# More weight slots, later stores of the low parts, and splits on GpSimd in a two-sequence encoder

## The chip, the cores and the metric

The kernel runs on one core of a Trainium2 chip. The metric is the device time of one execution, in microseconds. PE is TensorE, DVE VectorE, ACT ScalarE, POOL GpSimd, and SP is SyncE, which issues nearly all of this kernel's transfers.

## What is computed

Two sequences of 512 tokens, 1024 wide, go through the same two layers with the same weights.

```python
def encoder_trunk(x, p):
    for l in range(DEPTH):                                   # 2
        h = rms_norm(x, p['ln1_g'][l])
        z = h @ p['w_in'][l]                                 # 1024 -> 2816
        z_s5, z_hy, z_rw, z_na = jnp.split(z, IN_SPLITS, axis=-1)
        y_s5 = s5_mixer(z_s5, ...)                           # state-space scan
        y_hy = hyena_mixer(z_hy, ...)                        # long convolution
        y_rw = rwkv_mixer(z_rw, ...)                         # RWKV-7, both directions
        y_na = na_mixer(z_na, ...)                           # neighbourhood attention
        groups = [rms_norm(y, p['grp_g'][l, i]) for i, y in enumerate((y_s5, y_hy, y_rw, y_na))]
        x = x + jnp.concatenate(groups, axis=-1) @ p['w_out'][l]      # 1024 -> 1024
        h = rms_norm(x, p['ln2_g'][l])
        x = x + jnp.square(jax.nn.relu(h @ p['w_mlp1'][l])) @ p['w_mlp2'][l]   # 1024 -> 4096 -> 1024
    return x
y_prompt, y_sample = encoder_trunk(x_prompt, p), encoder_trunk(x_sample, p)
```

All of it is in float32.

## The kernel before

**Dense matmuls in three products.** A float32 operand is written as the sum of two numbers of the type fp32r, a high part and a low part. A dense product is then three matmuls, high by high, high by low and low by high (`mm3`: L1433 and L1434 read the weight's high part, L1435 its low part). `K.split` (L298 to L301) makes the parts: ScalarE casts the number to the high part (L300), and an engine that the caller names subtracts (L301) to get the low part.

**Weights come in tiles** of 512 by 128 numbers, 256 KB, 128 partitions by 512 elements in SBUF; one tile serves 12 matmuls of 512 columns. `load_w` (L1401) loads one. The first sequence meets each tile first: SyncE loads the raw tile into a low slot (L1419), ScalarE casts it into a high slot (L300), VectorE subtracts in place (L301), and SyncE stores the low part to DRAM (L1423). For the second sequence SyncE loads the raw tile (L1415) and the stored low part (L1416), and ScalarE casts in place (L1417). There are 376 tiles, so 376 first and 376 second loads. `NW` slots of 2 KB a partition hold them; the constants `NW, NHI = 7, 3` stand at L1835. A first load takes high slot `n % NHI` and low slot `NHI + n % (NW - NHI)`, a second load two slots in a ring over all `NW`; n counts loads.

**Activations** live in the rest of SBUF, `NMEM` units of 1 KB a partition, of which the dense stream has the first `DHI`; `DS5` bounds the S5 mixer's part (L1833). `Mem` hands out units and prefers ones that were freed long ago. `take` (L1707) splits a mixer's output into one tile of 8 units for each of the four groups, and `w_out` (L1544) reads them.

**Three streams of Python generators** write the program down side by side: the dense stream, the RWKV stream with S5 and the later mixers, and a first stream with preparation and the first mixers. The dense stream's order is: w_in of layer 0 for sequence 0 and for sequence 1; then for each layer and sequence w_out, MLP, and w_in of the next layer. While it works on one sequence, the mixers of the other run. A planner then lays out each engine's queue and SyncE's from these, by its own costs and by priorities; the dense matmuls have a lower priority than the mixers' (`OFF_P`). Each queue runs in that order. Semaphores are set from what the instructions read and write.

**Where the mixers touch this.** L442, L447 and L454 are GpSimd instructions of RWKV's preparation, the last of them ahead of the matmuls at L470. L551 makes the operands of the matmuls at L564, L668 scales RWKV's state, L959 and L604 are matmuls on data just loaded (S5's operands, RWKV's values). L1596 adds a matmul's result from PSUM to the MLP's sum, L1457 adds squares for a normalisation. `LO_V` (L1836) is not used.

Of the kernel before, what the change touches and what calls it, by code (L numbers as in the profile page):

```python
# [5 lines left out]
F32 = mybir.dt.float32  # L6
F32R = mybir.dt.float32r
# [5 lines left out]
P = 128  # L13
T = 1024
S = 512
# [1385 lines left out]
def load_w(K, key):  # L1401


    nc = K.nc
    sh = [P, 4, P]
    src = K.A[key[0]][key[1:]]
    n = K.nw
    K.nw += 1
    again = key in K.lows
    i, j = (2 * n % NW, (2 * n + 1) % NW) if again else (n % NHI, NHI + n % (NW - NHI))  # L1410
    hi, lo = (K.W.view(NMEM + 2 * o, sh, F32R) for o in (i, j))
    raw = K.W.view(NMEM + 2 * (i if again else j), sh, F32)
    K.tc.cur_priority -= OFF_W
    if again:
        nc.sync.dma_start(out=raw, in_=src)  # L1415
        nc.sync.dma_start(out=lo.bitcast(F32), in_=K.lows[key])  # L1416
        nc.scalar.copy(out=hi, in_=raw)  # L1417
    else:
        nc.sync.dma_start(out=raw, in_=src)  # L1419
        K.split(hi, lo, raw, nc.vector)  # L1420
        K.n += 1
        d = K.lows[key] = K.d(sh, f"lo_{K.n}")
        nc.sync.dma_start(out=d, in_=lo.bitcast(F32))  # L1423
    K.tc.cur_priority += OFF_W
    return hi, lo


def mm3(K, ps, terms):

    n = len(terms)  # L1430
    K.tc.cur_priority += OFF_P
    for i, (wh, wl, hh, hl) in enumerate(terms):
        K.nc.tensor.matmul(out=ps, lhsT=wh, rhs=hh, start=(i == 0), stop=False)  # L1433
        K.nc.tensor.matmul(out=ps, lhsT=wh, rhs=hl, start=False, stop=False)  # L1434
        K.nc.tensor.matmul(out=ps, lhsT=wl, rhs=hh, start=False, stop=(i == n - 1))  # L1435
    K.tc.cur_priority -= OFF_P


def dense(K, key, h, tag="pd"):

    w = [load_w(K, key + (kh,)) for kh in range(2)]
    ps = K.p([P, S], tag)
    mm3(K, ps, [(w[k // 4][0][:, k % 4], w[k // 4][1][:, k % 4], h[k][0], h[k][1]) for k in range(8)])
    return ps
# [99 lines left out]
def w_out(K, l, khs, ys, xsrc, xp, done, M):  # L1544


    nc = K.nc
    load = not xp
    for m in range(8):
        if load and m % 2 == 0:  # L1550
            xp.append(M([P, 2, S]))
        x = xp[m // 2][:, m % 2]
        if load:
            nc.sync.dma_start(out=x, in_=xsrc[m * P:m * P + P])
        w = [load_w(K, ('w_out', l, m, kh)) for kh in khs]
        ps = K.p([P, S], "pd")
        mm3(K, ps, [(w[i][0][:, j], w[i][1][:, j]) + tuple(ys[HALVES[kh][j // 2]][:, part, j % 2] for part in range(2))
                    for i, kh in enumerate(khs) for j in range(4)])
        nc.vector.tensor_tensor(out=x, in0=ps, in1=x, op=ADD)
        if done:  # L1560
            done(m, x, xp[m // 2])
        yield
    M.free(*(ys.pop(g) for kh in khs for g in HALVES[kh]))


def mlp(K, l, h, R2, xd, done, M):
# [15 lines left out]
    def second(e):  # L1582
        for m in range(8):
            if e == 0 and m % 2 == 0:
                acc.append(M([P, 2, S]))
            if e == 7 and m % 2 == 0:
                xp.append(M([P, 2, S]))
                nc.sync.dma_start(out=xp[-1], in_=xd[m * P:m * P + 2 * P].rearrange("(c p) t -> p c t", p=P))
            a = acc[m // 2][:, m % 2]
            wh, wl = load_w(K, ('w_mlp2', l, m, e))  # L1590
            ps = K.p([P, S], "pd")
            mm3(K, ps, [(wh[:, j], wl[:, j], hid[4 * e + j][:, 0], hid[4 * e + j][:, 1]) for j in range(4)])
            if e == 0:
                nc.scalar.copy(out=a, in_=ps)
            else:
                nc.vector.tensor_tensor(out=a, in0=ps, in1=a, op=ADD)  # L1596
            if e == 7:
                x = xp[-1][:, m % 2]
                nc.vector.tensor_tensor(out=a, in0=a, in1=R2, op=MUL)
                nc.vector.tensor_tensor(out=x, in0=a, in1=x, op=ADD)  # L1600
                done(m, x)
                if m % 2:
                    M.free(acc[m // 2], xp[-1])
            yield
        for j in range(4):
            M.free(hid.pop(4 * e + j))
# [46 lines left out]
def trunk(tc, A, O):  # L1653
    nc = tc.nc
    base = place(nc)
    with tc.tile_pool(name="sb", bufs=1) as sb, \
            tc.tile_pool(name="ps", bufs=1, space=bass.MemoryType.PSUM) as ps, \
            tc.tile_pool(name="dr", bufs=1, space=bass.MemoryType.DRAM) as dr:
        K = Ctx(tc, base, sb, ps, dr, A)
        K.s5w, K.hys, K.lows, K.nw, K.nz = {}, {}, {}, 0, 0  # L1660
        K.W = K.mem()

        DM, MX = K.mem((0, DHI)), K.mem((DHI, NMEM))
# [7 lines left out]
        zs, ys, taken, done = {}, {}, {}, set()  # L1671
# [19 lines left out]
        def into(l, b, h, st, DM):  # L1691
            R = norm_rstd(K, st, DM)
            zs[l, b] = (K.d([D, S], f"zr{b}", 2), K.d([16, 16, 8, 64], f"zd{b}", 2), K.d([768, S], f"zh{b}", 2),
                        K.d([768, S], f"zn{b}", 2))
            ys[l, b] = {}
            for i, _ in enumerate(w_in(K, l, pars[l], h, R, zs[l, b], FIRST[:] if l + b == 0 else None)):
                if i == 7:
                    done.add(("zr", l, b))
                    if b == 0 and l and len(ys[l - 1, 1]) == 4:
                        take(l - 1, 1)  # L1700
                    if b == 1 and l and len(ys[l, 0]) == 4:
                        take(l, 0)
                yield
            DM.free(*h)
            done.add(("z", l, b))

        def take(l, b, gs=range(4)):  # L1707

            t = taken.setdefault((l, b), {})
            for g in gs:  # L1710
                y, my = ys[l, b][g]
                t[g] = DM([P, 2, 2, S], F32R)
                K.split(t[g][:, 0], t[g][:, 1], y, nc.vector)
                my.free(y)
            if 2 in t:
                done.add(("freed", l, b))

        def layer(l, b):
# [10 lines left out]
            for khs in (((0,), (1,)) if l + b < SPL else ((0, 1),)):  # L1729
                gs = [g for kh in khs for g in HALVES[kh]]  # L1730
                while not all(g in ys[l, b] for g in gs):
                    yield
                if not done.issuperset([("freed", l, b)]):
                    take(l, b, gs)
                    yield
                yield from w_out(K, l, khs, taken[l, b], xs[l, b], x0, None if khs == (0,) else mid, DM)
# [93 lines left out]

NMEM, DHI, DLO, DS5 = 164, 84, 41, 144  # L1833

NW, NHI = 7, 3  # L1835
OFF_D, LO_V, MIX = 0, 4, 2  # L1836
FN, OFF_M, OFF_W, OFF_P, OFF_R = 2, 0, 0, 2000, 0
ACC_V, NF = 6, 4
# [1 line left out]
HALVES = ((1, 3), (0, 2))  # L1840
# [44 lines left out]
```

## Time and profile before

| | |
|---|---|
| median of 3 runs | 3182.41 us (3180.72 to 3187.07) |
| the profiled execution's own time | 3182.62 us |
| its span, first to last instruction | 3180.8 us |
| mean granted clock of TensorE, of 1 | 0.949 |
| PE busy | 2964.7 us, 93% |
| DVE busy | 1935.5 us, 61% |
| ACT busy | 1128.3 us, 35% |
| POOL busy | 453.6 us, 14% |
| DMA | 588.70 MB, 185 GB/s on the mean |

The span begins with the first instruction and ends with the last; 1.8 us of the execution lie outside it. A busy PE counts the time from a matmul's start to its modelled end, and matmuls overlap, so it is not PE at its peak. Stages are told apart by the weights that SyncE loads: the first load of w_out is issued at 464.19 us, of the MLP of layer 0 at 623.87 for the first sequence and at 1393.81 for the second, of w_out of layer 1 at 2109.79 and at 2742.85, of the MLP of layer 1 at 2211.59 and at 2816.53. The stages in the rows begin a little before these. [...]

### The profile page before, as it was taken

What the parts mean: (1) busy time and instruction counts of PE and PEld (TensorE: products, weight loads), DVE (VectorE), ACT (ScalarE), POOL (GpSimd) and SP (SyncE); (2) the same over time, 40 slices, a digit from 0 to 9 for tenths busy, and PEclk for the clock granted to TensorE, in tenths of its full rate; (3) what the DMA queues carried; (4) which work ended last, traced back from release to release, by engine and by line L of the source; (5) the groups of instructions that cost most, each with busy time, mean ns of one, the idle gap of its engine ahead of it and who ended that gap; (6) DMA issues with size and microseconds to landing.
All of it is one profiled execution on the core that took longest, in us unless ns stands there. A gap on an engine that the chain in (4) does not pass through costs nothing. (4 is left out here: it accounts for less than half of the span.)

```text
span 3180.8 us, 48627 instructions
## 1 busy us (share of the span) xinstructions
PE 2964.7 (93%) x17328; PEld 2317.7 (73%) x17328; DVE 1935.5 (61%) x3909; ACT 1128.3 (35%) x2080; POOL 453.6 (14%) x411
## 2 busy tenths in 40 slices
PE   7978999899999999999999899988999999799999
PEld 5666776677777867777777677866777777588887
DVE  7987783874874697653844527668547467731223
ACT  4333233443332343244332324333433333343332
POOL 3422210200100022211101002213000001100000
PEclk9988997899999999999999999989999999899999
DMA  7577564464565566774764655666646555466666
GB/s 220 184 228 189 172 188 142 139 169 158 163 194 168 188 204 202 240 236 155 207 174 145 182 169 196 218 200 187 177 139 169 174 178 185 155 215 194 194 192 215
DMA packets 491801, 588.70 MB, mean 185 GB/s; under 512 B 188678, under 2 KB 239494, under 8 KB 490536
## 3 DMA queue, kind: packets, MB, share of 16 engines
q1 hardware_dynamic: 491560, 585.59, 60.1%
q8 instruction: 139, 2.28, 0.3%
q14 instruction: 102, 0.84, 0.1%
HBM read 418.34 MB, written 164.22 MB: 183 GB/s over the span
## 5 line engine op out<-in xcount | busy, mean ns | idle before, releaser
L1433 PE MATMUL pd<-m,m 128*128 128x512 f32 x2984 | 1222.0, 410 | 63.8 <-ACT m L300 23.4
L1435 PE MATMUL pd<-m,m 128*128 128x512 f32 x2984 | 1205.7, 405 | 22.5 <-DMA m<-lo 15.7
L1434 PE MATMUL pd<-m,m 128*128 128x512 f32 x2984 | 1205.8, 404 | 1.6 <-DVE m L301 1.4
L1433 PEld LDWEIGHTS pd<-m,m 128*128 128x128 f32 x2984 | 578.3, 194 | 214.2 <-ACT m L300 27.8
L1435 PEld LDWEIGHTS pd<-m,m 128*128 128x128 f32 x2984 | 577.9, 194 | 166.3 <-DMA m<-lo 19.5
L1434 PEld LDWEIGHTS pd<-m,m 128*128 128x128 f32 x2984 | 579.1, 194 | 131.2 <-issue 8.4
L300 ACT CAST m<-m 128x512 fp32r<-128x512 f32 (+1 forms) x400 | 256.4, 644 | 619.9 <-PE pd L1434 220.6
L1417 ACT CAST m<-m 128x512 fp32r<-128x512 f32 x376 | 232.2, 619 | 612.9 <-DMA m<-in_w_mlp 362.4
L301 DVE TENSOR_TENSOR m<-m,m 128x512 fp32r<-128x512 f32 (+1 forms) x400 | 303.1, 761 | 203.4 <-ACT m L300 198.1
L1596 DVE TENSOR_TENSOR m<-pd,m 128x512 f32<-128x512 f32 x224 | 153.9, 688 | 205.4 <-PE pd L1435 204.5
L1578 DVE SCALAR_TENSOR_TENSOR do<-pd,do 128x512 f32<-128x512 f32 x128 | 88.0, 687 | 202.4 <-ACT do L1577 201.9
L1196 DVE TENSOR_TENSOR m<-m,m 128x512 f32<-128x512 f32 (+1 forms) x224 | 125.6, 601 | 6.5 <-PE ma L1375 4.8
L301 DVE TENSOR_TENSOR m<-do,m 128x512 fp32r<-128x512 f32 x128 | 88.2, 689 | 50.0 <-ACT m L300 49.2
L300 ACT CAST m<-do 128x512 fp32r<-128x512 f32 x128 | 79.4, 621 | 98.7 <-DVE do L1578 98.5
L1577 ACT ACTIVATE do<-pd 128x512 f32<-128x512 f32 x128 | 75.9, 593 | 37.6 <-PE pd L1435 37.3
L668 POOL TENSOR_TENSOR rw_se<-rw_st,rw_ec 128x256 f32<-128x256 f32 x24 | 15.8, 659 | 484.1 <-DVE rw_st L669 361.9
L470 PE MATMUL ra<-m,m 64*128 64x128 f32 x512 | 63.1, 308 | 21.8 <-DVE m L454 10.3
L1196 POOL TENSOR_TENSOR m<-m,m 128x512 f32<-128x512 f32 x32 | 49.0, 1534 | 234.7 <-DVE m L1196 77.7
L1457 POOL TENSOR_TENSOR m<-m 128x512 f32<-128x512 f32 x40 | 59.8, 1494 | 152.9 <-ACT m L1456 150.9
L863 POOL TENSOR_TENSOR m<-m,s5p_i 128x256 f32<-128x256 f32 x64 | 61.7, 963 | 135.7 <-DVE m L865 71.4
L678 PE MATMUL ra<-m,m 128*64 128x64 f32 x512 | 78.8, 248 | 1.3 <-DVE m L653 0.9
L470 PEld LDWEIGHTS ra<-m,m 64*128 64x128 f32 x512 | 54.3, 206 | 34.9 <-issue 24.3
(363 smaller groups left out, 3505.6 us busy)
## 6 DMA issues: line engine op xcount, KB each, us to landing
m<-in_w_mlp SPq DMA_DIRECT2D x512, 256.0 KB, 2.9
lo<-m SPq DMA_DIRECT2D x376, 256.0 KB, 2.6
m<-lo SPq DMA_DIRECT2D x376, 256.0 KB, 2.7
m<-in_w_in SPq DMA_DIRECT2D x176, 256.0 KB, 3.2
m<-zr SPq DMA_DIRECT2D x36, 512.0 KB, 4.8
m<-in_w_out SPq DMA_DIRECT2D x64, 256.0 KB, 3.5
m<-in_xT SPq DMA_DIRECT2D x32, 256.0 KB, 4.3
zr<-do SPq DMA_DIRECT2D x32, 256.0 KB, 2.4
```

The costliest lines, as they stand in the source:

```text
L300: self.nc.scalar.copy(out=hi, in_=x)
L301: eng.tensor_tensor(out=lo, in0=x, in1=hi.bitcast(F32), op=SUB)
L470: nc.tensor.matmul(out=pm[q][:, ch - c2, c], lhsT=bk[c][h, ch].rearrange("p a b -> p (a b)"), rhs=ar[c][h, ch].rearrange("p a b -> p (a b) ...
L678: nc.tensor.matmul(out=py[b0:b0 + 64, d, c], lhsT=uv[:, ch, c, q], rhs=sr[:, ch, 2 * c + q], start=st is None, stop=True)
L1196: eng.tensor_tensor(out=o, in0=a, in1=b, op=op)
L1417: nc.scalar.copy(out=hi, in_=raw)
L1433: K.nc.tensor.matmul(out=ps, lhsT=wh, rhs=hh, start=(i == 0), stop=False)
L1434: K.nc.tensor.matmul(out=ps, lhsT=wh, rhs=hl, start=False, stop=False)
L1435: K.nc.tensor.matmul(out=ps, lhsT=wl, rhs=hh, start=False, stop=(i == n - 1))
L1577: nc.scalar.activation(out=r, in_=ps, func=AF.Relu)
L1578: nc.vector.scalar_tensor_tensor(out=r, in0=ps, scalar=0.0, in1=r, op0=MAX, op1=MUL)
L1596: nc.vector.tensor_tensor(out=a, in0=ps, in1=a, op=ADD)
```

## The change

It has four parts. The weights get eleven slots instead of seven, four of them for high parts; the activations get 8 units less, all of them from the dense stream's region. The store of a low part is no longer written right behind its split but after the load of the tile two later; before a second load all pending stores are written. The subtraction of a first load goes to GpSimd in three of four cases. And a mixer's output is split into two tiles of 4 units instead of one of 8.

```diff
     K.tc.cur_priority -= OFF_W
     if again:
+        store_lows(K)
         nc.sync.dma_start(out=raw, in_=src)
         nc.sync.dma_start(out=lo.bitcast(F32), in_=K.lows[key])
         nc.scalar.copy(out=hi, in_=raw)
     else:
         nc.sync.dma_start(out=raw, in_=src)
-        K.split(hi, lo, raw, nc.vector)
-        K.n += 1
-        d = K.lows[key] = K.d(sh, f"lo_{K.n}")
-        nc.sync.dma_start(out=d, in_=lo.bitcast(F32))
+        K.split(hi, lo, raw, nc.vector if K.nw % LO_V == 0 else nc.gpsimd)
+        K.late.append((key, lo))
+        store_lows(K, 2)
     K.tc.cur_priority += OFF_W
     return hi, lo
+
+def store_lows(K, n=0):
+    while len(K.late) > n:
+        key, lo = K.late.pop(0)
+        K.n += 1
+        d = K.lows[key] = K.d([P, 4, P], f"lo_{K.n}")
+        K.nc.sync.dma_start(out=d, in_=lo.bitcast(F32))
...
-        mm3(K, ps, [(w[i][0][:, j], w[i][1][:, j]) + tuple(ys[HALVES[kh][j // 2]][:, part, j % 2] for part in range(2))
+        mm3(K, ps, [(w[i][0][:, j], w[i][1][:, j]) + tuple(ys[HALVES[kh][j // 2]][part][:, j % 2] for part in range(2))
...
-    M.free(*(ys.pop(g) for kh in khs for g in HALVES[kh]))
+    M.free(*(t for kh in khs for g in HALVES[kh] for t in ys.pop(g)))
...
-        K.s5w, K.hys, K.lows, K.nw, K.nz = {}, {}, {}, 0, 0
+        K.s5w, K.hys, K.lows, K.late, K.nw, K.nz = {}, {}, {}, [], 0, 0
...
-                t[g] = DM([P, 2, 2, S], F32R)
-                K.split(t[g][:, 0], t[g][:, 1], y, nc.vector)
+                t[g] = [DM([P, 2, S], F32R) for _ in range(2)]
+                K.split(*t[g], y, nc.vector)
...
-NMEM, DHI, DLO, DS5 = 164, 84, 41, 144
+NMEM, DHI, DLO, DS5 = 156, 76, 41, 136
...
-NW, NHI = 7, 3
+NW, NHI = 11, 4
 OFF_D, LO_V, MIX = 0, 4, 2
```

## Rows read from the trace of the kernel before

**Rows 1.** By stage: busy us (x instructions) of PE, PEld, DVE, ACT, POOL; clock; DMA.
```profile
460.00:622.00 162.00, 149.81 (x1104) 111.78 (x1103) 96.14 (x214) 60.69 (x131) 17.12 (x18) 0.80 0.50 146
622.00:1154.00 532.00, 501.82 (x3207) 392.00 (x3206) 350.94 (x689) 185.75 (x353) 57.04 (x47) 0.97 0.58 175
...
1394.00:1937.00 543.00, 515.68 (x3136) 390.26 (x3137) 271.27 (x527) 189.49 (x341) 56.92 (x52) 0.96 0.60 179
...
2108.00:2210.00 102.00, 83.23 (x514) 68.35 (x513) 91.92 (x225) 32.28 (x55) 29.39 (x20) 0.85 0.59 188
2210.00:2740.00 530.00, 506.34 (x3143) 394.68 (x3142) 324.04 (x609) 188.90 (x367) 41.44 (x41) 0.97 0.57 172
2740.00:2815.00 75.00, 56.00 (x254) 46.26 (x253) 41.80 (x76) 20.21 (x32) 12.56 (x9) 0.84 0.55 173
2815.00:3180.00 365.00, 359.69 (x1589) 296.59 (x1587) 98.83 (x145) 123.89 (x209) 1.29 (x1) 1.00 0.62 200
sum 3180.00, PE 2964.72 PEld 2317.70 DVE 1935.47 ACT 1128.25 POOL 453.59; mean PE 247.06 PEld 193.14 DVE 161.29 ACT 94.02 POOL 37.80
```

**Rows 2.** TensorE's waits, whole span: us in total, times, longest.
```profile
PE pd L1433 <- ACT m L300: 23.4, 9, 12.3
PE ra L564 <- DVE m L551: 20.8, 7, 4.4
PE pd L1435 <- DMA m<-lo: 15.7, 9, 3.8
...
PE ma L959 <- DMA m<-s_sB: 11.7, 5, 4.9
...
PE ra L470 <- DVE m L454: 10.3, 5, 6.3
...
PE ra L470 <- DVE m L453: 7.5, 6, 4.0
...
PE pd L1435 <- DVE m L301: 6.7, 5, 3.3
PE pd L1433 <- ACT m L1417: 6.4, 1, 6.4
...
PE ra L604 <- DMA m<-zr: 2.8, 2, 1.5
```

**Rows 3.** TensorE's waits in the stage 0 to 207.
```profile
PE pd L1433 <- ACT m L300: 12.3, 1, 12.3
```

**Rows 4.** SyncE's own waits, whole span.
```profile
SPq L1416 <- PE pd L1434: 628.0, 274, 27.2
SPq L1419 <- PE pd L1435: 372.3, 199, 6.8
SPq L1423 <- DVE m L301: 274.3, 226, 6.2
```

**Rows 5.** Waits of all engines, whole span.
```profile
DVE m L301 <- ACT m L300: 247.3, 189, 7.0
ACT m L300 <- PE pd L1434: 220.6, 102, 9.4
```

**Rows 6.** Line L301: duration ns min/median/max, first and last start.
```profile
L301 DVE TENSOR_TENSOR m<-m,m x400: 654/690/1836, 16.1 to 2777.9; 128x512 fp32r<-128x512 f32 x127, 128x1024 fp32r<-128x1024 f32 x7
```

**Rows 7.** Line L1596, the same columns.
```profile
L1596 DVE TENSOR_TENSOR m<-pd,m x224: 662/691/702, 756.9 to 3175.6; 128x512 f32<-128x512 f32 x112
```

**Rows 8.** Line L1457, the same columns.
```profile
L1457 POOL TENSOR_TENSOR m<-m x40: 1267/1456/2404, 6.5 to 2816.2; 128x512 f32<-128x512 f32 x40
```

**Rows 9.** GpSimd's groups by line: busy us, mean ns, idle before.
```profile
L447 POOL TENSOR_TENSOR m<-m,m 128x512 f32<-128x512 f32 x16 | 29.9, 1871 | 14.4 <-DVE m L445 11.5 <-ACT m L431 2.9
L454 POOL TENSOR_TENSOR m<-m,m 64x512 f32<-64x512 f32 x16 | 24.5, 1529 | 1.3
L442 POOL TENSOR_TENSOR m<-m,m 128x512 f32<-128x512 f32 x16 | 24.2, 1514 | 87.5 <-ACT m L431 87.4
```

**Rows 10.** DMA issues: count, KB each, median us to landing.
```profile
xm<-m SPq DMA_DIRECT2D x32, 256.0 KB, 4.3
```

## The prediction

> **What bounds the kernel now.** I read the table by stage first [rows 1]. The line of sums shows TensorE busy for 2964.7 of 3180 us, VectorE for 1935.5, ScalarE for 1128.3, GpSimd for 453.6: TensorE is the bound, and all that better supply can give back is its idle time of 215 us, plus what the clock loses where it is below 1.00. The rows above the sums say where that lies. The first sequence's MLP of layer 0 (622 to 1154) takes 532 us and the second's (1394 to 1937) 543, although the first does the splits and the second reads finished low parts: how the low parts are made does not set the pace of an MLP, because mixers of another pair of sequence and layer share TensorE with it. The last MLP, alone on the engine, takes 365 us. Three stages have idle time and a low clock together: 460 to 622 (clock 0.80), 2108 to 2210 (0.85) and 2740 to 2815 (0.84). There the dense work is short and the mixers' chains run bare.
>
> Then the waits of TensorE by releaser [rows 2]. Those that a weight ends are short: 23.4 us for a high part of a first load, 15.7 for a low part read back, 6.7 for a low part from the split, 6.4 for a high part of a second load. Of the first, 12.3 us is a single wait in the opening stage [rows 3], when nothing is loaded yet; slots cannot help it. The mixers' own waits stand beside them: 20.8 us at L564, 10.3 and 7.5 at L470, and 11.7 and 2.8 for mixer data still being loaded.
>
> The queue that issues the loads looks much worse than what reaches TensorE [rows 4]: SyncE waits 628.0 us to issue the read of a low part until the slot's last matmul is over, 372.3 to issue a first load for the same reason, and 274.3 us at L1423 until the split that it is to store is done. Behind each of these waits stand all later transfers, the mixers' too. In the engines' queues the same shows [rows 5]: VectorE idles 247.3 us before a split until ScalarE has made the high part, and ScalarE idles 220.6 us before that cast until matmuls free a high slot. So the chain load, cast, split, store is tight, but TensorE mostly has other work in front of it meanwhile.
>
> **The change, part by part.**
>
> *Eleven slots.* A second load uses two of them, so 5.5 tiles fit where 3.5 did; a first load has 4 high and 7 low slots instead of 3 and 4. A tile is 12 matmuls; in the last MLP 128 tiles take 365 us, 2.85 us each [rows 1]. Two more tiles ahead are 5.7 us of lead. Against that stand the second sequence's waits, 15.7 + 6.4 = 22.1 us [rows 2]. I take all of it: -22; the bounds are -22 and 0 (if the wait merely moves to the next thing in TensorE's queue). For the first sequence the waits are 23.4 - 12.3 + 6.7 = 17.8 us [rows 2, 3]. The fourth high slot loosens the cast, but the split becomes longer (below), so I take half: -9, between -18 and 0.
>
> *Stores two tiles later.* The same 376 stores are issued, each behind the load of the tile after the next. SyncE no longer holds at a split that is only just starting, so of the 274.3 us most goes; the waits for a slot's matmul stay, though with seven low slots they start later [rows 4]. What TensorE sees of this queue is late mixer data: 11.7 + 2.8 = 14.5 us [rows 2]. I take half: -7, between -14.5 and 0. The low slot is held longer by the late store, which three more slots cover; the memory in DRAM is read back a whole stage later. These two I cost at nothing; without the extra slots each load would wait for a store two tiles on.
>
> *Splits on GpSimd.* 376 splits are first loads; their numbers start at multiples of four, so exactly 282 move. VectorE has a median of 690 ns for this line [rows 6], so it is relieved of 282 x 0.690 = 195 us. GpSimd's addition of the same form has a median of 1456 ns and a minimum of 1267 [rows 8], so it takes on 282 x 1.456 = 411 us (at least 357) and goes from 454 to about 865 us, 27% of the span. In the stage 2210 to 2740, 96 of 128 splits move: 140 us more, on top of 41.4, is 181 of 530 us, about a third [rows 1]. Behind a split that waits for its cast now stand GpSimd's mixer instructions. Nearest to TensorE are the three ahead of L470: L442, L447 and L454, sixteen of each [rows 9]. I estimate that half of the sixteen rounds fall beside first-sequence stages. If each of these instructions met one split, that is 8 x 3 x 1.456 = 35 us; by the third of the time that GpSimd is busy, 12 us. I take +12, between 0 and +35.
>
> VectorE's relief should shorten the mixers' chains: waits on VectorE at L564 and L470 are 20.8 + 10.3 + 7.5 = 38.6 us [rows 2], and it would no longer stand 247.3 us before splits [rows 5]. But the two engines are not independent. The same split line has a median of 690 ns and a maximum of 1836 on VectorE [rows 6], while additions that read one operand from PSUM stay between 662 and 702 in all 224 cases [rows 7]; GpSimd's additions spread from 1267 to 2404 [rows 8]. Something makes an instruction with both inputs in SBUF wait up to 1.15 us, about one GpSimd instruction. So I cost this at nothing, between -19 (half of the 38.6) and +19: the 195 us that VectorE saves stand against up to 411 us in which its two-input instructions may be shut out.
>
> [...]
>
> *Less room for activations.* The dense stream's region goes from 84 units to 76. The fullest moment is the end of an output projection: 32 units of mixer output, 32 of normalised activations, 4 for the statistics and 4 for a pair of x tiles, 72 in all, which fits, with one spare pair instead of three. New x pairs then land where an older pair was just stored, and a store takes 4.3 us [rows 10]. Twelve pairs in three such stages are 52 us at worst, but the loads are issued ahead of their matmuls, which cover them; I cost this at nothing, and it widens the range upwards. Splitting the mixer output into two tiles each changes no instruction's work.
>
> *Order.* The program's planner lays out every queue from its own costs, so all queues are laid out anew. I have no row for that; the clock can go either way by half of what it loses in the three bare stages: 162 x 0.20 + 102 x 0.15 + 75 x 0.16 = 60 us [rows 1], so 30 us to either side.
>
> **Sum.** -22 - 9 - 7 + 12 = -26 us. The profiled execution took 3182.6 us, 1.8 outside its span, and the median of the runs is 3182.4, the same. 3182.6 - 26 = 3156.6: I predict 3157 us.
>
> **Rivals.**
>
> *GpSimd becomes the hold-up (slower).* Place: the first sequence's stages, where GpSimd's splits sit in front of L442, L447 and L454 and shut VectorE out of its two-input work. Then the 35 us come whole, the 9 us for the first sequence do not come, and the 38.6 us of mixer waits on VectorE grow by half, +19: -22 - 7 + 35 + 19 = +25, 3208 us. It decides from the point where GpSimd costs TensorE more than the 22 + 7 = 29 us that slots and queue give. For it: the maxima in [rows 6, 8]. Against it: GpSimd has two thirds of its time left, and VectorE no longer stands before splits.
>
> *Nothing comes of it.* TensorE's queue is in fixed order; a weight that comes earlier lets it arrive earlier at a mixer matmul that is not ready, and the idle time changes its name. For it: the two MLP stages of 532 and 543 us. Then about 3183 us.
>
> *The bare stages shrink.* If mixers finish earlier because VectorE is freed, the three stages named lose half their idle time, (12.2 + 18.8 + 19.0) / 2 = 25 us, and half the clock loss, 30 us; 7 of it is the late mixer data counted above: -26 - 55 + 7 = -74, 3109 us. For it: TensorE's longest mixer waits are on VectorE [rows 2]. Against it: the second of the stages has splits of its own, on the slower engine.
>
> **Numbers.** The forecast's case gets 0.40, with 3135 to 3175 as its own range; GpSimd as hold-up 0.28; nothing 0.13; the bare stages 0.19. A difference of 0.2% (6 us) is about what a measurement of this kernel can tell from no change. Faster by more than that: 0.40 + 0.19 = 0.59; within it 0.13; slower 0.28. The range reaches from somewhat under the third rival to just over the first, 3100 to 3212; outside are all gains together with a better clock, and a hold-up on GpSimd together with late x pairs or a worse clock.
>
> **What the profile of the changed kernel would show.** If the steps are right: the waits for low parts read back and for L1417 all but gone from TensorE's list; SyncE's wait at the store under 100 us; VectorE busy about 195 us less, GpSimd about 411 more, at some 1.45 us a split; L470's waits on GpSimd longer by about 12 us. If GpSimd is the hold-up: TensorE waits for a low part from GpSimd, splits well over 1.5 us, VectorE's two-input lines with a higher mean than now. The prediction is wrong if TensorE's idle time does not fall though the weight waits do, or if the clock in the three bare stages moves by more than a tenth.

## The result, and the profile after

The changed kernel takes 3212.1 us in the median of four runs (3206.7 to 3219.4) against 3184.7 us for four runs of the kernel before, timed beside it: a ratio of 1.0072, with a 95% interval of 1.0048 to 1.0095. It is slower by 0.7%. The forecast was 3157 us, so the time moved the other way; the rival that ends nearest is the one with GpSimd as the hold-up, 3208 us.

First the table by stage of the changed kernel, with the columns of [rows 1]; the borders are set where its stages begin. Left out are four stages.

```profile
210.00:440.00 230.00, 204.80 (x1394) 159.27 (x1394) 155.84 (x349) 74.37 (x142) 50.44 (x52) 0.90 0.66 189
440.00:690.00 250.00, 190.63 (x1364) 145.89 (x1362) 172.53 (x402) 73.20 (x154) 54.48 (x45) 0.73 0.42 115
690.00:1241.00 551.00, 518.76 (x3288) 404.03 (x3288) 330.77 (x634) 192.83 (x373) 193.78 (x153) 0.97 0.56 172
...
1490.00:2034.00 544.00, 527.20 (x3302) 411.03 (x3300) 278.06 (x574) 195.63 (x382) 53.11 (x51) 0.95 0.58 175
...
2217.00:2273.00 56.00, 51.36 (x416) 40.16 (x417) 30.23 (x45) 23.02 (x46) 19.85 (x15) 0.94 0.88 272
2273.00:2790.00 517.00, 500.00 (x2963) 394.20 (x2961) 288.00 (x508) 179.49 (x344) 178.53 (x139) 0.98 0.54 170
2790.00:2841.00 51.00, 47.77 (x200) 38.26 (x199) 31.14 (x38) 19.09 (x30) 8.31 (x6) 0.97 0.82 273
2841.00:3212.00 371.00, 365.36 (x1615) 301.43 (x1613) 100.75 (x147) 125.03 (x211) 2.58 (x2) 1.00 0.62 198
sum 3212.00, PE 2974.15 PEld 2327.53 DVE 1874.64 ACT 1130.42 POOL 834.22; mean PE 247.85 PEld 193.96 DVE 156.22 ACT 94.20 POOL 69.52
```

Set beside [rows 1], the loss has one place. The first MLP begins at 690 us where it began at 622. The stage ahead of it, the first output projection, takes 250 us instead of 162; TensorE idles 59 us in it (250.0 - 190.6) where it idled 12, and its clock is 0.73 instead of 0.80. From there to the end the changed kernel is faster: 3212 - 690 = 2522 us against 3180 - 622 = 2558. So 68 us are lost before the first MLP and 36 won behind it. The two other bare stages have all but gone (102 to 56 us, 75 to 51). TensorE's idle time over the whole span is 3212.0 - 2974.2 = 238 us, up from 215.

TensorE's waits in the changed kernel, with the columns of [rows 2]. L1442 to L1444 are the lines that were L1433 to L1435; all later lines have moved by 9.

```profile
PE pd L1442 <- DVE do L1587: 32.7, 16, 6.3
PE pd L1442 <- DVE m L1605: 20.1, 14, 4.0
PE ma L959 <- DMA m<-s_gd: 14.9, 1, 14.9
PE pd L1442 <- ACT m L300: 13.6, 3, 12.5
...
PE ma L959 <- DMA m<-s_sB: 9.9, 6, 3.3
PE pd L1444 <- DMA m<-lo: 9.9, 1, 9.9
...
PE ra L564 <- DVE m L551: 7.9, 4, 3.9
PE ra L470 <- DVE rsq_xma L275: 6.5, 1, 6.5
...
PE ra L470 <- DVE rsq_tma L251: 4.3, 1, 4.3
...
PE ra L470 <- DVE m L454: 3.2, 1, 3.2
...
PE ra L470 <- DVE m L475: 2.9, 4, 1.2
...
PE pd L1443 <- DVE m L301: 2.7, 2, 1.8
...
PE pd L1442 <- ACT m L1418: 2.1, 1, 2.1
...
PE ra L470 <- DVE m L453: 1.8, 1, 1.8
```

The waits for weights did shrink: for a second load 9.9 + 2.1 = 12.0 us instead of 22.1, for a first load 13.6 - 12.5 = 1.1 instead of 17.8, once the opening wait is taken off. (The 2.7 us at L1443 are no weight's: that line reads the weight's high part and the low part of an activation.) Of the mixers' waits on VectorE those at L564 fell from 20.8 to 7.9 us. Those at L470 only changed their releaser: 6.5 + 4.3 + 3.2 + 2.9 + 1.8 = 18.7 us, where 10.3 + 7.5 and 1.1 behind L475 made 18.9. TensorE waits nowhere for a split on GpSimd. Yet its idle time rose: no wait on the prediction's list explains the slower time.

The two longest rows are not on that list. Matmuls of the MLP wait there for VectorE's L1587 and L1605, which read the MLP's results out of PSUM: 52.8 us, where the same lines, L1578 and L1596, made 14.3 + 4.8 = 19.1 before. No single part of the change accounts for them: they are 22.8 + 6.2 = 29.0 us in splits_dve and 9.6 + 10.1 = 19.7 us in slots7, two kernels of the next section.

SyncE's own waits after the change, with the columns of [rows 4]:

```profile
SPq L1417 <- PE pd L1443: 522.2, 249, 13.4
SPq L1420 <- PE pd L1444: 392.4, 204, 26.0
SPq L1434 <- POOL m L301: 284.6, 198, 4.4
SPq L1417 <- PE pd L1444: 88.6, 44, 4.5
SPq L1434 <- DVE m L301: 70.1, 49, 5.8
```

The wait at the store (now L1434) is 284.6 + 70.1 = 354.7 us in these two rows, and the prediction had it under 100. The 274.3 us of [rows 4] are no fit counterpart: the same line has many more rows there, under other releasers (25.7 us behind a weight's load, 15.9 and 14.7 behind VectorE's L516 and L515). Added up over the 197 longest rows of all SyncE waits, the store's line waits 406.9 us before and 393.3 after, and all lines together 2090.6 and 2090.0.

What is late shows in three timelines: the start in us, the duration, the engine and the line. First the kernel before. L1227 are transforms of Hyena on TensorE, in the mixer of layer 0 and sequence 0, and L1196 the additions on their results on VectorE. Hyena's first pass has two groups of both; the first is early in both kernels (additions at 176.4 us before, at 194.7 after), and the rows show the second. SyncE's L1331 loads a bias for the neighbourhood attention, the next mixer, for the second time; L1419 is the first load of the first MLP.

```profile
284.99 1.13 PE L1227 MATMUL ma<-m,m 128*128 128x256 f32 x4
...
288.90 1.28 DVE L1196 TENSOR_TENSOR m<-ma,m 128x512 f32<-128x512 f32 x2
...
480.41 0.33 SPq L1331 DMA_DIRECT2D m<-in_na_bias  x1
...
623.87 2.88 SPq L1419 DMA_DIRECT2D m<-in_w_mlp  x2
```

The same lines of the changed kernel, with RWKV's preparation (L442, L440) between them:

```profile
280.27 1.13 PE L1227 MATMUL ma<-m,m 128*128 128x256 f32 x4
...
391.71 1.23 POOL L442 TENSOR_TENSOR m<-m,m 128x512 f32<-128x512 f32 x1 [5.91 <-ACT m L431]
...
394.66 1.17 DVE L440 SCALAR_TENSOR_TENSOR m<-m,m 128x256 f32<-128x256 f32 x2
...
398.04 1.27 DVE L1196 TENSOR_TENSOR m<-ma,m 128x512 f32<-128x512 f32 x2
...
580.73 0.34 SPq L1331 DMA_DIRECT2D m<-in_na_bias  x1
...
692.51 0.89 SPq L1420 DMA_DIRECT2D m<-in_w_mlp  x2
```

These transforms are done some 5 us earlier than before, but the addition on their results starts 117 us later (398.0 against 280.3 + 1.1), right behind instructions of RWKV, another mixer in another stream. The two share no data. What they share is found in the addresses.

**The cause, as a theory (M, memory).** The first mixers, Hyena and then the attention, take their tiles from the units `DLO` to `DHI`, and only when these are full from `DHI` to `NMEM`, where RWKV and S5 live:

```
DS, MW = K.mem((0, DLO)), K.mem((DLO, DHI), (DHI, NMEM))
MR, MS = K.mem((DHI, DS5), (DS5, NMEM), tight=True), K.mem((DS5, NMEM), (DHI, DS5))
```

With `DHI` at 84 their own part has 84 - 41 = 43 units, with `DHI` at 76 it has 35. The addresses that the program hands out, listed while it is built, are these: of the 120 tiles of this stream none lay in the shared part before, and 14 do after the change. Twelve are Hyena's small tiles, one belongs to Hyena's spectra, and one is the attention's bias. Some of them (unit, size, the new tile | the tile that held the unit last):

```
108 2 return M([P, 2, 256])     | ep_ = M([P, 8, 128])            (RWKV, L428)
132 2 return M([P, 2, 256])     | t = M([P, n, S])                (RWKV's loads, L324)
104 2 return M([P, 2, 256])     | b_t = M([P, 8, 2, 64])          (RWKV, L438)
 92 2 return M([P, 2, 256])     | wp = M([P, 2, 2, S], F32R)      (RWKV's weights, L375)
 76 6 bias = M([P, 3, 2, 256])  | sa, sr = M([P, 8, 4, 64]), ...  (RWKV's state, L460)
```

L440 and L442 are the readers of `ep_`. So Hyena would wait until RWKV has read a tile of its own out, a write after a read; the attention's bias, on RWKV's state tile, would be loaded after RWKV's end (L1331 at 580.7 instead of 480.4), and the first output projection, which needs both mixers, would starve. The trace agrees with the second wait too: the last matmul that reads that state tile (L678) starts at 580.4 us. But the bias of the first pass, which did not spill, is as late (507.6 us instead of 410.1), so in the changed kernel the two waits run side by side.

**The rival (G, GpSimd)** is the one from the prediction: 282 subtractions that take longer and stand in front of mixer work make RWKV and Hyena late. The time of 3208 us speaks for it, and so does the stage, in which first loads and mixers run together.

### The profile page after: what moved, and what is told of

Its sections match the earlier page's. It is cut to its first block, busy times and chain, and to the rows that moved or that the text cites. A ratio compares the mean times of both kernels' runs of the same rounds, so it can differ in the third digit from the quotient of the medians.

```text
span 3212.0 us, 48748 instructions
## 1 busy us (share of the span) xinstructions
PE 2974.2 (93%) x17328; PEld 2327.5 (72%) x17328; DVE 1874.6 (58%) x3627; ACT 1130.4 (35%) x2082; POOL 834.2 (26%) x693
## 5 line engine op out<-in xcount | busy, mean ns | idle before, releaser
L1442 PE MATMUL pd<-m,m 128*128 128x512 f32 x2984 | 1216.1, 408 | 92.4 <-DVE do L1587 32.7
L1444 PE MATMUL pd<-m,m 128*128 128x512 f32 x2984 | 1201.7, 403 | 10.1 <-DMA m<-lo 9.9
L1443 PE MATMUL pd<-m,m 128*128 128x512 f32 x2984 | 1202.6, 403 | 5.1 <-DVE m L301 2.7
L1442 PEld LDWEIGHTS pd<-m,m 128*128 128x128 f32 x2984 | 575.5, 193 | 248.3 <-issue 45.7
L1444 PEld LDWEIGHTS pd<-m,m 128*128 128x128 f32 x2984 | 575.2, 193 | 143.7 <-DMA m<-lo 10.4
L1443 PEld LDWEIGHTS pd<-m,m 128*128 128x128 f32 x2984 | 577.0, 193 | 134.3 <-issue 10.0
L301 POOL TENSOR_TENSOR m<-m,m 128x512 fp32r<-128x512 f32 x282 | 396.7, 1409 | 711.1 <-ACT m L300 630.0
L1605 DVE TENSOR_TENSOR m<-pd,m 128x512 f32<-128x512 f32 x224 | 153.6, 687 | 220.2 <-PE pd L1444 219.6
L1587 DVE SCALAR_TENSOR_TENSOR do<-pd,do 128x512 f32<-128x512 f32 x128 | 87.9, 687 | 266.1 <-ACT do L1586 265.7
L301 DVE TENSOR_TENSOR m<-m,m 128x512 fp32r<-128x512 f32 (+1 forms) x118 | 107.2, 909 | 75.9 <-ACT m L300 54.1
L1196 DVE TENSOR_TENSOR m<-m,m 128x512 f32<-128x512 f32 (+1 forms) x224 | 143.5, 685 | 1.4 <-POOL m L1196 0.6
L301 DVE TENSOR_TENSOR m<-do,m 128x512 fp32r<-128x512 f32 x128 | 96.6, 755 | 60.3 <-ACT m L300 59.9
L470 PE MATMUL ra<-m,m 64*128 64x128 f32 x512 | 67.5, 318 | 19.6 <-DVE rsq_xma L275 6.5
L470 PEld LDWEIGHTS ra<-m,m 64*128 64x128 f32 x512 | 57.2, 216 | 36.2 <-issue 25.0
L678 PE MATMUL ra<-m,m 128*64 128x64 f32 x512 | 80.8, 253 | 0.6 <-DVE m L653 0.3
L1473 DVE SCALAR_TENSOR_TENSOR m<-m,par,m 128x512 fp32r<-128x512 f32 x64 | 66.5, 1049 | 24.9 <-ACT m L1472 24.8
```

Source lines behind the costliest of these rows:

```text
L301: eng.tensor_tensor(out=lo, in0=x, in1=hi.bitcast(F32), op=SUB)
L470: nc.tensor.matmul(out=pm[q][:, ch - c2, c], lhsT=bk[c][h, ch].rearrange("p a b -> p (a b)"), rhs=ar[c][h, ch].rearrange("p a b -> p (a b) ...
L678: nc.tensor.matmul(out=py[b0:b0 + 64, d, c], lhsT=uv[:, ch, c, q], rhs=sr[:, ch, 2 * c + q], start=st is None, stop=True)
L1196: eng.tensor_tensor(out=o, in0=a, in1=b, op=op)
L1587: nc.vector.scalar_tensor_tensor(out=r, in0=ps, scalar=0.0, in1=r, op0=MAX, op1=MUL)
```

## Experiments

All ratios are to the kernel before, on the same chip, with 95% intervals. "First MLP" is the first SyncE row of the MLP's weights, "Hyena" the first start of VectorE's L1196 on two SBUF operands in the source view; before, these are 623.9 and 290.1 us, after the change 692.5 and 401.3. "Low parts" says where the subtractions of first loads run.

| kernel | slots | DLO, DHI | stores | low parts | ratio | first MLP | Hyena |
|---|---|---|---|---|---|---|---|
| the change | 11 | 41, 76 | late | GpSimd | 1.0072 (1.0048 to 1.0095) | 692.5 | 401.3 |
| mem_only | 7 | 41, 76 | at once | VectorE | 1.0181 (1.0157 to 1.0205) | 708.6 | 407.6 |
| own_part | 7 | 49, 84 | at once | VectorE | 1.0165 (1.0131 to 1.0199) | 710.3 | 410.4 |
| splits_dve | 11 | 41, 76 | late | VectorE | 1.0029 (1.0010 to 1.0048) | 690.1 | 397.3 |
| overflow_s5 | 11 | 41, 76 | late | GpSimd | 1.0031 (1.0012 to 1.0050) | 669.5 | 291.1 |
| slots7 | 7 | 41, 84 | late | GpSimd | 0.9972 (0.9952 to 0.9992) | 601.0 | 276.2 |
| late_only | 7 | 41, 84 | late | VectorE | 1.0020 (1.0003 to 1.0036) | 629.5 | 291.6 |
| pool_only | 7 | 41, 84 | at once | GpSimd | 0.9999 (0.9979 to 1.0020) | 615.2 | 283.0 |
| eight_dve | 8 | 41, 84 | late | VectorE | 0.9985 (0.9965 to 1.0006) | 625.5 | 285.1 |
| ten_slots | 10 | 41, 80 | late | GpSimd | 0.9954 (0.9936 to 0.9973) | 611.3 | 289.3 |
| first_on_dve | 10 | 41, 80 | late | GpSimd, not the first 44 | 0.9986 (0.9964 to 1.0008) | 620.9 | 285.9 |
| slots_only | 10 | 41, 80 | at once | VectorE | 0.9916 (0.9885 to 0.9946) | 621.1 | 288.4 |
| ten_dve | 10 | 41, 80 | late | VectorE | 0.9858 (0.9829 to 0.9886) | 622.3 | 286.9 |

**mem_only: the smaller memory alone.** The kernel before, with the mixer output in two tiles and

```diff
-NMEM, DHI, DLO, DS5 = 164, 84, 41, 144
+NMEM, DHI, DLO, DS5 = 156, 76, 41, 136
```

> The kernel before with the smaller activation memory alone: 156 units, 76 of them the dense stream's, mixer outputs split into two tiles; seven slots, stores and splits as before. Theory M (memory: the first mixers' own part falls from 43 to 35 units, so Hyena of layer 0, sequence 0 gets units of RWKV's and waits for RWKV): the first load of the MLP of layer 0 moves from 624 us to about 690, the clock of the stage before it falls to about 0.75, and the total is about 3215 us. Theory G (GpSimd's splits hold the mixers up): nothing of this, 3183 us.

Measured: 3254.3 us, 1.8% slower, with the first MLP at 708.6 and Hyena at 407.6. The loss of the whole change, and more (60 us, about twice what was expected), comes with the constants alone; neither a slot nor GpSimd was touched.

**slots7: everything but the slots and the memory.**

```diff
-NMEM, DHI, DLO, DS5 = 156, 76, 41, 136
-NW, NHI = 11, 4
+NMEM, DHI, DLO, DS5 = 164, 84, 41, 144
+NW, NHI = 7, 3
```

> The changed kernel with seven slots and the memory of before, so late stores and splits on GpSimd alone. Theory M: no bare stretch before the MLP of layer 0, whose first load is near 620 us, and a total of 3150 to 3185 us. Theory G: about 3205 us or more, with the MLP of layer 0 still late.

Measured: 3184.7 us, ratio 0.9972, first MLP at 601.0. With the memory back GpSimd's 282 subtractions make nothing late.

**ten_slots: the change with one slot less, and 4 units given back** to the dense region. A slot is 2 units, so slots and activations together take 20 + 160 = 180 units, where the change takes 22 + 156 and the kernel before 14 + 164, 178 each.

```diff
-NMEM, DHI, DLO, DS5 = 156, 76, 41, 136
-NW, NHI = 11, 4
+NMEM, DHI, DLO, DS5 = 160, 80, 41, 140
+NW, NHI = 10, 4
```

> The changed kernel with ten slots and 160 units, 80 of them the dense stream's: the first mixers' own part is 39 units, which holds all their tiles. Everything else as in the changed kernel. Theory M: the MLP of layer 0 begins near 620 us and the total falls to 3140 to 3170 us. Theory G: one slot less changes nothing good, about 3210 us.

Measured: 3178.0 us, ratio 0.9954, first MLP at 611.3; the time falls short of the range expected. The own part has 39 units and none of its 120 tiles spills. Four units turn a loss of 0.7% into a gain of 0.5%.

**splits_dve: the change without GpSimd.**

```diff
-        K.split(hi, lo, raw, nc.vector if K.nw % LO_V == 0 else nc.gpsimd)
+        K.split(hi, lo, raw, nc.vector)
```

> The changed kernel with all splits back on VectorE; eleven slots, late stores and the small memory stay. Theory M: the MLP of layer 0 still begins near 690 us, total 3195 to 3225 us. Theory G: near 3157 us, since GpSimd is relieved.

Measured: 3203.4 us, ratio 1.0029. The first MLP stays at 690.1 and Hyena at 397.3. GpSimd is gone from the splits and the lateness is not: G falls as its cause. GpSimd does cost something, 1.0072 against 1.0029.

**own_part: only the first mixers' part is smaller.** M says that the dense stream's room does not matter. So here `DHI`, `NMEM` and the slots stay, and the dense stream in layer 0 is even given 8 units more:

```diff
-NMEM, DHI, DLO, DS5 = 164, 84, 41, 144
+NMEM, DHI, DLO, DS5 = 164, 84, 49, 144
```

> The kernel before with one number changed: the border between sequence 1's first activations and the first mixers' own part at unit 49 instead of 41, so that part has 35 units of the same 84. Nothing else of the change. Theory M: the same loss as with the small memory: first load of layer 0's MLP near 700 us, total 3230 to 3255 us. Rival R (the dense stream's smaller region is what costs, by later x pairs and hidden tiles): 3183 us, since the dense stream keeps its 84 units.

Measured: 3245.8 us, ratio 1.0165. The listing again shows 14 of 120 tiles in the shared part. Its timeline repeats the picture of the changed kernel, RWKV's L442 and then Hyena's L1196:

```profile
403.44 1.10 POOL L442 TENSOR_TENSOR m<-m,m 128x512 f32<-128x512 f32 x1
...
408.61 1.27 DVE L1196 TENSOR_TENSOR m<-ma,m 128x512 f32<-128x512 f32 x2
...
710.34 0.38 SPq L1419 DMA_DIRECT2D m<-in_w_mlp  x1
```

and its table by stage the starved output projection, 77 us idle at a clock of 0.73:

```profile
444.00:710.00 266.00, 188.97 (x1366) 141.76 (x1364) 181.03 (x435) 78.11 (x162) 40.87 (x37) 0.73 0.42 113
```

This is one number in the kernel before, and it moves the time more than the whole change did. (The number also gives the dense stream's opening 8 units more, so the run by itself does not tell a spill from a tighter own part; overflow_s5, next, does.) It also warns against reading the 36 us behind the first MLP as the slots' gain: here 3239.6 - 710.3 = 2529 us remain, 28 less than before, with no slot added. Part of what the late start costs comes back by itself: the two later bare stages take 60 and 45 us in own_part instead of 102 and 75. That the mixers are further on when the dense stream gets to them is the likely reason; no run tests it.

**overflow_s5: the same 14 tiles on other neighbours.** The spill goes to S5's units first:

```diff
-        DS, MW = K.mem((0, DLO)), K.mem((DLO, DHI), (DHI, NMEM))
+        DS, MW = K.mem((0, DLO)), K.mem((DLO, DHI), (DS5, NMEM), (DHI, DS5))
```

> The changed kernel, eleven slots and all, with one line different: what does not fit the first mixers' own 35 units goes to S5's part first instead of RWKV's. The same 14 tiles overflow, but none lands on a tile of RWKV. Theory M in its narrow form (the wait is for RWKV's tiles): MLP of layer 0 begins between 610 and 650 us and the total is 3150 to 3185 us. If any overflow costs as much, it stays near 690 and 3212 us.

Measured: 3202.6 us, ratio 1.0031; the gain that was expected came only in part. The instructions are those of the changed kernel, GpSimd's too; only addresses differ. Hyena has the same 35 units of its own and starts on time, at 291.1: it had waited for RWKV's memory. But the attention's bias now lies on S5's input tile, and its load waits for S5's end:

```profile
289.93 1.28 DVE L1196 TENSOR_TENSOR m<-ma,m 128x512 f32<-128x512 f32 x2
...
574.29 0.34 SPq L1331 DMA_DIRECT2D m<-in_na_bias  x1
...
669.46 0.38 SPq L1420 DMA_DIRECT2D m<-in_w_mlp  x1
```

S5's last reader, VectorE's L1053, ends just before, at 574.15 (573.04 + 1.11). So it is not the count of spilled tiles that sets the loss but whose tile lies there, and when it is let go. Hyena's wait and the attention's wait are now told apart in part: moving Hyena's away won 23 us at the first MLP. The 46 us that stay go with the attention's wait, whose bias is 94 us late; no run takes that wait away alone.

**late_only: late stores alone**, with seven slots and the old memory (the line of splits_dve and the constants of slots7):

> Late stores alone (and mixer outputs as two tiles): seven slots, 164 units, splits on VectorE. By my sum -7 us: about 3176. If late stores give what the seven-slot run gave, the splits on GpSimd give nothing; if they give more, the splits on GpSimd cost the difference.

Measured: ratio 1.0020, first MLP at 629.5. By themselves late stores bring nothing here.

**pool_only: GpSimd alone**, at seven slots. As slots7, and

```diff
-        store_lows(K, 2)
+        store_lows(K)
```

> Splits on GpSimd alone (and mixer outputs as two tiles): seven slots, 164 units, stores right behind the splits. By my sum +12 us less what VectorE's relief gives, which I had at nothing: about 3195. Theory G puts it at 3208 or above.

Measured: ratio 0.9999 (0.9979 to 1.0020). By itself the move to GpSimd changes nothing that can be told.

**ten_dve: ten slots, late stores, all low parts on VectorE** (ten_slots with the line of splits_dve).

> Ten slots with 160 units as in the earlier run, late stores, all splits on VectorE. Theory M with GpSimd as a cost: w_in of layer 0 for sequence 0 ends near 183 us as with eleven slots and VectorE, no bare stretch before layer 0's MLP, total 3140 to 3165 us, better than ten slots with GpSimd. If GpSimd's relief of VectorE pays, it is slower than that run.

Measured: 3149.9 us, ratio 0.9858. It is the best version here: 1.4% under the kernel before and, by the two ratios, 0.9858 / 1.0072 = 0.979, 2.1% under the changed one. Its first MLP starts where that of the kernel before does; the gain comes later, 3158.2 - 622.3 = 2536 us against 2557. (The traces show 21 us and the ratio 45: this trace is of the longest of ten_dve's four runs, 3160.1 us, and the one before is of a run of 3182.6 us, where the runs beside ten_dve have a median of 3195.2.)

**slots_only: ten slots alone** (ten_dve with the store right behind the split).

> Ten slots and 160 units alone: stores right behind the splits, splits on VectorE, mixer outputs as two tiles. Set beside the run with late stores too (0.9858 of the kernel before) it tells what late stores add when there is room for them. By my sum slots give -31 us of -38: about 0.990. If the stores matter more once slots are there, it stays at 0.995 or above.

Measured: 3164.3 us, ratio 0.9916, some 27 us. In size that is near what the prediction had added up for slots, 22 + 9 = 31.

**first_on_dve: where does GpSimd's cost arise?** As ten_slots, but the first projection's 44 subtractions stay on VectorE:

```diff
+        K.split(hi, lo, raw, nc.vector if K.nw % LO_V == 0 or K.nw <= 44 else nc.gpsimd)
```

> Ten slots, late stores, three of four splits on GpSimd except for the first 44 tiles, which stay on VectorE. If the price of GpSimd lies in w_in of layer 0 beside S5's preparation, this is as fast as ten slots with all splits on VectorE (0.986). If it is spread over all first-sequence stages, it stays near ten slots with GpSimd (0.995).

Measured: 0.9986 (0.9964 to 1.0008), not better than ten_slots. Either expectation is missed; that GpSimd's price lies in the opening stage alone is refuted.

**eight_dve: eight slots in the old memory** (four high, four low; all else as ten_dve).

> Eight slots (four for high parts) with the full 164 units, late stores, splits on VectorE. If depth of slots is what pays, it lies between seven slots (late stores alone: 1.002) and ten (0.986). If the loss of activation memory is what still costs at ten, it is faster than ten.

Measured: 0.9985 (0.9965 to 1.0006). That is 0.35% less than late_only, which has one slot fewer, with intervals that overlap; the gain comes between eight and ten.

## Why the prediction was wrong

**The step that failed** is "Less room for activations. ... I cost this at nothing". It counted the fullest moment of the dense stream, 72 of 76 units, and found it to fit, which it does. It did not ask who else has `DHI` as a border, and so had a wait at nothing that the kernel then had: the first mixers' wait for RWKV's tiles. The constant is also the upper end of the first mixers' own part, so 8 units less there made 14 tiles spill into memory of a mixer that runs at the same time. Measured, the term is +53 us (own_part, 1.65% of 3195) to +58 us (mem_only, 1.81% of 3194) where the sum had 0. With all other parts in place it is of the same size: splits_dve against ten_dve, which differ in the memory and one slot, are 1.0029 / 0.9858 = 1.017, 55 us. That the spilled tiles are the cause is shown by own_part, where neither slots, stores, GpSimd nor `DHI` changes, by overflow_s5, where the same tiles in other places give Hyena its start back, and by ten_slots and ten_dve, in which nothing spills.

**Slots.** -31 us forecast, about -27 measured (slots_only, at ten slots). The size came out; the path is not shown. In slots_only TensorE's waits for weights fell by 20 us (second loads from 22.1 to 7.3 + 2.3 = 9.6, first loads from 17.8 to 17.6 - 11.9 + 4.8 = 10.5), but its idle time did not: 3159.9 - 2940.0 = 219.9 us in that trace, 216.1 before. What this pair of traces has to show for the gain is a shorter busy time of TensorE, 2940.0 instead of 2964.7 us, for which the slots' term has no place. As far as these traces go, the idle time changed its name, as the second rival said. So the size is no evidence for the step, and may be luck.

**Stores two tiles later.** -7 us forecast. At ten slots 0.9858 against 0.9916, -0.6% with intervals that just touch; at seven slots +0.2%. The step's picture was wrong: SyncE's wait at the store did not go away. Over all releasers it is 406.9 us before and 393.3 after, and with the loads 1503.2 and 1445.5 us; the prediction had read only the largest row of that line, 274.3 us. SyncE's waits of all lines add up to the same 2090 us: it waits at one place instead of another.

**GpSimd.** +12 us forecast; it depends on what stands around it: +0.43% (14 us) at eleven slots, +0.97% (31 us) at ten, nothing alone, and at seven slots with late stores 0.9972 against 1.0020, a gain. Each rebuilding lays out all queues anew, and the runs do not tell a price of the engine from a price of the layout. This stays open. What they do show is how little VectorE got from it. The source view of the changed kernel, with the columns of [rows 6]; L1605 answers to [rows 7]:

```profile
L301 POOL TENSOR_TENSOR m<-m,m x282: 1257/1291/3028, 13.4 to 2794.2; 128x512 fp32r<-128x512 f32 x141
...
L1605 DVE TENSOR_TENSOR m<-pd,m x224: 654/691/727, 833.4 to 3206.7; 128x512 f32<-128x512 f32 x112
```

Two groups of the changed kernel's page, with the columns of [rows 9] (busy us, mean ns):

```profile
L1196 DVE TENSOR_TENSOR m<-m,m 128x512 f32<-128x512 f32 (+1 forms) x224 | 143.5, 685 | 1.4 <-POOL m L1196 0.6
L301 DVE TENSOR_TENSOR m<-do,m 128x512 fp32r<-128x512 f32 x128 | 96.6, 755 | 60.3 <-ACT m L300 59.9
```

The same two groups of the page before:

```profile
L1196 DVE TENSOR_TENSOR m<-m,m 128x512 f32<-128x512 f32 (+1 forms) x224 | 125.6, 601 | 6.5 <-PE ma L1375 4.8
L301 DVE TENSOR_TENSOR m<-do,m 128x512 fp32r<-128x512 f32 x128 | 88.2, 689 | 50.0 <-ACT m L300 49.2
```

GpSimd took on 834.2 - 453.6 = 381 us, near the 411 of the prediction (1.35 us more for each of 282). VectorE should have lost 195 us and lost 1935.5 - 1874.6 = 61. Most of the difference, 134 us, was given back in instructions that stayed. Added up over the two traces, the durations of L301's `m<-m,m` on VectorE fell from 304.6 to 107.3 us, those of VectorE's instructions with a tile in PSUM were 644.0 and 643.6 us, and those of all its others rose from 1188.2 to 1297.4 us, by 109. (Durations of neighbours overlap a little; the busy time counts such a stretch once.) In the mean the two groups above, with two operands in SBUF, grew from 689 to 755 ns and from 601 to 685; the line of [rows 7], with one in PSUM, had 688 and 687. Three pairs that differ in the move alone, or nearly, show the same growth of the two groups: 697 to 755 and 633 to 685 ns (splits_dve to the change), 691 to 746 and 594 to 668 (ten_dve to ten_slots), 689 to 759 and 601 to 675 (the kernel before to pool_only).

The trace of the changed kernel shows one by one which instructions grew:

```profile
880.38 1.46 POOL L301 TENSOR_TENSOR m<-m,m 128x512 fp32r<-128x512 f32 x1 [3.41 <-ACT m L300]
880.68 1.72 DVE L301 TENSOR_TENSOR m<-do,m 128x512 fp32r<-128x512 f32 x1
```

Of VectorE's 222 instructions of 128x512 at L301, 26 took over 750 ns, up to 1887. Each of them starts while GpSimd is in an instruction, and ends 545 to 554 ns after that one; the 190 that start outside GpSimd's instructions took at most 695 ns. At L1605, with one operand in PSUM, 35 of 224 start during an instruction of GpSimd, and none of the 224 took more than 727 ns. By what the one kind is held up and the other is not, no run shows. The prediction's choice to cost VectorE's relief at nothing fits these numbers.

**The rivals.** GpSimd as the hold-up gave 3208 us and the run 3212, but for another reason: its sign would have been the weights' gain eaten by L442, L447 and L454, and splits_dve, without GpSimd, has the same late MLP. "The bare stages shrink" came true in its two later stages (102 to 56, 75 to 51 us) and not in its sum. Its reason, a freed VectorE, is not the cause, since own_part, which moves no split, has it too (60 and 45 us): it goes with a late first MLP. The prediction's own test, idle time that does not fall though the weight waits do, is what happened; so did the other, a clock in a bare stage that moves by more than a tenth (0.84 to 0.97 ahead of the last MLP).

**What stays open:** why late stores help at ten slots and not at seven, GpSimd's price apart from the layout, and by what path more slots shorten the run. Mixer outputs in two tiles were never run by themselves; pool_only, which has them, is at 0.9999. Eleven slots with an own part in which nothing spills were not tried; with 160 units they would take 182 units.

## What to carry to other kernels

When a constant that divides memory is moved, list every pool that has it as a border and count the tiles that spill, before anything is costed; whether the fullest consumer still fits is only one of the questions. A tile that lands on another stream's memory is a wait for that stream's progress, and here it showed as an engine that starts long after its input is ready (VectorE's L1196, 117 us after its transforms), behind an instruction that shares no data with it. And take the last slot only if the room that it needs is free: ten slots won 0.8% by themselves, while the eleventh came with a spill that cost more than everything else brought. When waits are added up by releaser, add all rows of a line: one releaser's row can shrink while its neighbours grow.

## What the runs showed of the hardware

Moving a two-operand SBUF instruction from VectorE to GpSimd freed VectorE of only about a third of it here: 61 of 195 us. The instructions on VectorE with both operands in SBUF got longer (L301's group on `do` has a mean of 724 to 768 ns in the six kernels with the move, and 689 to 697 in three without: the kernel before, splits_dve and ten_dve), while L1596, L1605 after the change, which reads PSUM, kept its mean: 688 and 687 ns. In the starved first output projection the granted clock fell too: it was 0.73 with TensorE idle for 59 of 250 us, and 0.80 before the change with 12 of 162 us. The idle share alone does not set it: from 1322 to 1394 us of the kernel before TensorE idled 11.5 of 72 us at 0.95.
